# Three z buffers in turn from the y projections on, and operand groups of out and up made from z instead of DRAM

## The chip, the cores and the metric

The kernel runs on one core of a Trainium2 chip. The metric is device time in microseconds (us) of one execution; the median over several runs counts. An execution with the hardware profiler switched on gives the profile and the trace. The core's engines are TensorE (PE, with its weight loads as PEld), VectorE (DVE), ScalarE (ACT), GpSimd (POOL) and SyncE (SP). Each works through its own list of instructions in order, and they wait for one another with semaphores. SP, ACT and POOL also issue transfers (DMAs).

## The reference

One residual block over x of 512 tokens by 2048 channels, float32. What the change touches is the middle:

```python
y_m = hm @ w_branch_m                       # 1024 -> 2048
y_c = (cb * causal_dwconv(cc * ch, conv_w)) @ w_branch_c
merged = sigmoid(gm_pre) * y_m + sigmoid(gc_pre) * y_c
h = h + merged @ w_out                      # 2048 -> 2048

hn = rmsnorm(h, norm_ffn_g)
u = causal_dwconv(hn @ w_up, ffn_conv_w, ffn_conv_b)   # 2048 -> 2 * 5504
gate, val = jnp.split(u, 2, axis=-1)
h = h + (silu(gate) * val) @ w_down         # 5504 -> 2048
return rmsnorm(h, norm_out_g)
```

Before it stand the input projections (q, k, v, gates, the convolution's three inputs, gm_pre and gc_pre) and the mLSTM that gives hm.

## The kernel before

**Products and steps.** Channels lie on the 128 partitions, the 512 tokens along the row. Every matrix product is made of *items*. An item is one pair of output blocks (2 x 128 channels by 512 tokens) and has nq *steps*; a step takes in four blocks of 128 input channels, as two *cells* of two blocks each. A cell is a 2 x 2 block product (two input blocks, two output blocks or token halves of 256) done with seven block products instead of eight. Each block product is three matmuls, because every operand is split into a high part and a low rest (hi*hi + hi*lo + lo*hi). So a cell has 21 matmuls of 128x128 by 128x256 (lines 229 to 231), a step 42.

**Operand groups.** The activations of a cell are an *operand group*: `cell_task` loads two blocks from DRAM into a raw tile (L267, L268), makes the sums that the seven products need (t3, e, t4: L276, L281, L286; for up also the scaling by the norm's weights, L273 and L274), and writes the high part (L290, ScalarE) and the low rest (L293, VectorE) into one of eight group tiles. Weights go the same way in `weight_task`: a load of five transfers a step (three on SP, two adding ones on POOL at L204), two sums (L169, L174), high parts (L184, ScalarE) and low rests (`wl`, L188, VectorE). Raw tiles of weights and groups share a ring of six.

**Banks and z.** The seven products go to four banks of PSUM: three of the item's own set (two sets, in turn), and half of one bank, P_BANK, that both sets share. At an item's end `evac_first` (L245, ScalarE) copies P_BANK to a part of the item's buffer z, and in the next step four VectorE operations (L251 to L254) add up the rest there. z has two buffers, zs[0] and zs[1], that items take in turn:

```python
it.set = it.num % 2
it.z = zs[it.set]
```

The next item's first matmul into P_BANK waits for the copy before it.

**Posts.** What an item does with z afterwards is its post, in one to four pieces with a cost each. Pieces wait in a list, `posts`. Each step adds 5.04 us to a credit and takes off the VectorE work in it; at the end of a step the list is worked off as far as the credit goes, or at once when the first piece belongs to an *urgent* item. `flush(n)` issues all pieces up to item n. At the end of item n the main loop does this:

```python
flush(it.num - 2)
if it.pre:
    it.pre(it)
evac_first(it)
```

`pre` loads a second operand for the post into mA or mB (L628): gc_d for y_c, gm_d for y_m, xT for out, the residual for down; up has none. Stores to DRAM that a post makes are collected in `late` and issued by ScalarE (L146): right after a flush, else in the next step.

**Order.** Items follow in the order x (40 items of 4 steps, the input projections), y_c and y_m (8 items of 2 steps each), out (8 of 4), up (43 of 4), three parts of down (8 each, of 4, 3 and 3), and a last stage for the remaining channels. In each the last two items, and from y_c on the first two, are interleaved step by step. `phase` gives every group the step at which it must be complete (`spread`, relative to the stage's first step, and not before `after`); its sums run two steps earlier and its low rest one step earlier.

**The middle.** A y_c item's post multiplies z by the gate and stores it in mc_d. A y_m item's post multiplies z by its gate (L660), loads mc_d into the buffer z2 (L659), adds it (L663), negates the second half (L665: the products give minus the second block) and stores the pair in m_d. The groups of out load from m_d. An out item's post adds x (`residual`, L672 and L673), stores h_d and squares (L684); the squares are summed in z2 (L688), and after the last item summed over channels (L332) and turned into the norm's factor `rstd` (L340, L343). The groups of up load from h_d.

Of the kernel before, what the change touches and what calls it, by code (L numbers as in the profile page):

```python
# [11 lines left out]
AF = mybir.ActivationFunctionType  # L12
# [31 lines left out]
def kpair(c):  # L44

    q, r = divmod(c, 2)
    return 4 * q + r, 4 * q + 2 + r


class Item:  # L50


    def __init__(self, load, nq, xs, post, pre=None):
        self.load, self.nq, self.xs, self.post, self.pre = load, nq, xs, post, pre
        self.p1_start, self.urgent = True, False
        self.set = self.num = self.z = self.buf = None


class Task:


    def __init__(self, load, sums, hi, lo, ready=None):
        self.load, self.sums, self.hi, self.lo, self.ready = load, sums, hi, lo, ready
        self.wh = self.wl = None
        self.raw, self.cost, self.plain = None, (0.8, 2.05), False


@with_exitstack
def tile_block(ctx: ExitStack, tc: tile.TileContext, xT, w1, w_v0, w_v1, w_v2, w_bm, w_bc, w_out, w_up, w_down,
# [62 lines left out]
    gm_d, gc_d, mc_d, m_d, h_d, h2_d = (D_([KD, P, T], s) for s in ("gm_d", "gc_d", "mc_d", "m_d", "h_d", "h2_d"))  # L132
    a_d = D_([NF, P, T], "a_d")
    gates_d = D_([P, T], "gates_d")
    stored = set()
# [121 lines left out]
    def cell_task(xs, c, d, scale=None, key=None):  # L257

        k1, k2 = kpair(c) if isinstance(c, int) else c
        t = Task(None, None, None, None)  # L260

        def new_raw():
            t.raw = wp.tile([P, NW], F32, tag="raw", name=nm("xraw"), bufs=RAW)

        def load():
            new_raw()
            SP.dma_start(t.raw[:, 5 * SW:], d[k1])  # L267
            SP.dma_start(t.raw[:, :2 * SW], d[k2])  # L268

        def t3():  # L270
            x = slots(t.raw)
            if scale:
                A.activation(t.raw[:, 5 * SW:], t.raw[:, 5 * SW:], AF.Copy, scale=scale(k1))  # L273
                A.activation(t.raw[:, :2 * SW], t.raw[:, :2 * SW], AF.Copy, scale=scale(k2))  # L274

            V.tensor_sub(x[:, 2:4], x[:, 1:6:4], two(x[:, 6]))  # L276

        def e():

            x = slots(t.raw)  # L280
            V.scalar_tensor_tensor(x[:, 4], x[:, 3], -1.0, x[:, 1], op0=ALU.mult, op1=ALU.subtract)  # L281

        def t4():

            x = slots(t.raw)
            V.scalar_tensor_tensor(x[:, 6], x[:, 4], -1.0, x[:, 0], op0=ALU.mult, op1=ALU.subtract)  # L286

        def hi():
            t.act = actp.tile([P, 2 * NW], F32R, tag="act", name=nm("act"))
            A.activation(t.act[:, :NW], t.raw, AF.Copy)  # L290

        def lo():
            V.tensor_sub(t.act[:, NW:], t.raw, f(t.act[:, :NW]))  # L293
            t.raw = None
            xs[t.cell] = t.act
            t.act = None

        t.load, t.sums, t.hi, t.lo, t.new_raw = load, [t3, e, t4], hi, lo, new_raw
        t.cost = (1.35, 1.95)
        t.ready = (lambda: all(k in stored for k in key)) if key else None  # L300
        return t


# [349 lines left out]

    def ym_post(p):
        def post(it):
            j1, j2 = kpair(p)

            def one():
                SP.dma_start(sb_pair(z2), pair_ap(mc_d, j1, j2))  # L659
                V.tensor_mul(it.z, it.z, it.buf[:, :2 * T])  # L660

            def two_():
                V.tensor_add(it.z, it.z, z2)  # L663
                b = it.z[:, T:]
                A.activation(b, b, AF.Copy, scale=-1.0)  # L665
                store(pair_ap(m_d, j1, j2), sb_pair(it.z), ("m", p))
            return [(1.2, one), (1.2, two_)]
        return post

    def residual(it):  # L670
# [1 line left out]
        V.tensor_add(a, it.buf[:, :T], a)  # L672
        V.tensor_sub(b, it.buf[:, T:2 * T], b)  # L673

    acc = z2

    def out_post(p):
        def post(it):
            j1, j2 = kpair(p)

            def one():
                residual(it)
                store(pair_ap(h_d, j1, j2), sb_pair(it.z), ("h", p))
                A.activation(acc if p == 0 else it.buf[:, :2 * T], it.z, AF.Square)  # L684

            def two_():
                if p:
                    V.tensor_add(acc, acc, it.buf[:, :2 * T])  # L688
                if p == 7:
                    cols, rows_pe, rows_post = rows_stages(SIDE, rstd, mC)  # L690
                    side.append((lambda: sum_tokens(SIDE, acc, 2, 4, True, True), cols))
                    side.append((rows_pe, rows_post))
            return [(1.3, one), (1.2, two_)]
        return post

    def up_post(j):
# [38 lines left out]
    def add(items, inter):  # L735

        i = 0
        while i < len(items):
            n = 2 if i in inter else 1
            group = items[i:i + n]  # L740
            if n == 2:
                group[1].p1_start = False
            for it in group:
                it.num = len(items_all)
                it.set = it.num % 2
                it.z = zs[it.set]
                items_all.append(it)
            for q in range(group[0].nq):
                for it in group:
                    steps.append((it, q))  # L750
            i += n

    def phase(items, xs, cells, first_pair=True, last_pair=True, chained=False):

        inter = ({0} if first_pair else set()) | ({len(items) - 2} if last_pair else set())
        e = len(steps)
        add(items, inter)
        for n, t in enumerate(cells):
            t.cell, t.e, t.xs = n, e, xs
            if n == 7 and chained:  # L760
                for it in items_all[-len(items) - 2:-len(items)]:
                    it.urgent = True
            t.after = e + n - 2 if chained and n > 5 else 0
            t.spread = e + ((-4, -2, -1, 0, 2, 3, 5, 6) if items[0].nq > 2 else (-4, -2, 0, 1))[n]
            use = [s for s in range(e, len(steps)) if steps[s][1] == n // 2]
            t.first, t.last = use[0], use[-1]
            all_cells.append(t)
# [24 lines left out]
    def x_task(c):  # L792
# [20 lines left out]
        def hi():  # L813
# [7 lines left out]

    YC, HM, MM, HH = {}, {}, {}, {}
    phase([Item(tiles_load(w_bc, *kpair(p)), 2, YC, yc_post(p), load_pair(gc_d, *kpair(p))) for p in range(8)],
          YC, [cell_task(YC, c, yc_d, None, [("yc", k) for k in kpair(c)]) for c in range(4)])
    phase([Item(tiles_load(w_bm, *kpair(p)), 2, HM, ym_post(p), load_pair(gm_d, *kpair(p))) for p in range(8)],
          HM, [cell_task(HM, c, hm_d, None, [("hm", k) for k in kpair(c)]) for c in range(4)])
    phase([Item(tiles_load(w_out, *kpair(p)), 4, MM, out_post(p), load_pair(xT, *kpair(p))) for p in range(8)],
          MM, [cell_task(MM, c, m_d, None, [("m", c)]) for c in range(8)], chained=True)

    def up_load(j):  # L830
        return tiles_load(w_up, j, NF + j)

    phase([Item(up_load(j), 4, HH, up_post(j)) for j in range(NF)],
          HH, [cell_task(HH, c, h_d, g_ffn, [("h", c)]) for c in range(8)], chained=True)

    for c, (k0, nq) in enumerate(CHUNKS):
        AA = {}
# [67 lines left out]

    e_last = len(steps)
    t = last_act()
    t.cell, t.e, t.first, t.last, t.after, t.spread, t.xs = "x", e_last, e_last, e_last + 15, 0, 0, plain
    all_cells.append(t)
    n_main = len(steps)  # L910
    steps.extend((l, 0) for l in lasts)
# [5 lines left out]
    for n, t in enumerate(all_cells):  # L917
        if n < 8:
            k = t.cell // 2
        else:  # L920
            k = max(k, all_cells[n - 8].last + 3, t.e - 4, t.after, t.spread)
# [50 lines left out]
    def flush(upto):  # L972

        if posts and posts[0][2] <= upto:
            while posts and posts[0][2] <= upto:
                posts.popleft()[1]()
        flush_late()


    hf_tiles = {}  # L980
# [136 lines left out]
    for s in range(4, len(steps)):  # L1117
# [69 lines left out]
        for fn in dmas:  # L1187
            fn()
        if main and q == it.nq - 1:
            flush(it.num - 2)  # L1190
            if it.pre:
                it.pre(it)
            evac_first(it)
            ended.append(it)
        if t2 and not t2.plain:
            t2.hi(1)
# [1 line left out]
            fn()  # L1198
        if s >= 4 + hold:
            credit = min(credit, 2.5)  # L1200
            while posts and (credit > posts[0][0] / 2 or posts[0][2] in urgent or not main):
                cost, fn, _ = posts.popleft()
                credit -= cost
                fn()
# [84 lines left out]
```

## Time and profile before

| what | value |
|---|---|
| median of 3 runs | 2841.49 us (2838.44 to 2846.11) |
| the profiled execution | 2842.29 us, span 2840.5 us |
| TensorE busy | 2606.6 us, 92% of the span |
| VectorE busy | 2213.0 us, 78% |
| ScalarE busy | 1294.4 us, 46% |
| GpSimd busy | 853.8 us, 30% |
| granted TensorE clock, mean | 0.963 |
| moved by DMA | 642.36 MB, 226 GB/s |

The span is the time from the first to the last instruction; the execution's own time is a little longer. Busy time is a union over an engine's instructions. In the profile a group of instructions is a line, an engine, an operation and the tiles written and read; a wait is the idle time of an engine before an instruction, put down to what ended it.

### The profile page before, as it was taken

What the parts mean: (1) busy time and instruction counts of PE and PEld (TensorE: products, weight loads), DVE (VectorE), ACT (ScalarE), POOL (GpSimd) and SP (SyncE); (2) the same over time, 40 slices, a digit from 0 to 9 for tenths busy, and PEclk for the clock granted to TensorE, in tenths of its full rate; (3) what the DMA queues carried; (4) which work ended last, traced back from release to release, by engine and by line L of the source; (5) the groups of instructions that cost most, each with busy time, mean ns of one, the idle gap of its engine ahead of it and who ended that gap; (6) DMA issues with size and microseconds to landing.
All of it is one profiled execution on the core that took longest, in us unless ns stands there. A gap on an engine that the chain in (4) does not pass through costs nothing.

```text
span 2840.5 us, 55407 instructions
## 1 busy us (share of the span) xinstructions
PE 2606.6 (92%) x20868; PEld 2578.5 (91%) x20868; DVE 2213.0 (78%) x3360; ACT 1294.4 (46%) x1623; POOL 853.8 (30%) x1003
## 2 busy tenths in 40 slices
PE   7899999999999776689799999999999989979798
PEld 6899999999999776689799999999999979979797
DVE  5777768877777775777879988888888887767676
ACT  6444544455544332344545444444444443434343
POOL 3343323333332221132233333333333223222320
PEclk9999999999999888799999999999999999989899
DMA  7799998989898887798788888989888789889886
GB/s 189 177 236 239 235 245 204 248 214 251 225 240 224 229 238 217 205 259 232 220 211 223 221 225 221 227 216 227 221 223 223 203 227 258 235 236 251 225 244 202
DMA packets 504254, 642.36 MB, mean 226 GB/s; under 512 B 46849, under 2 KB 327425, under 8 KB 503985
## 3 DMA queue, kind: packets, MB, share of 16 engines
q1 hardware_dynamic: 326512, 451.78, 50.4%
q0 software_dynamic: 141536, 125.09, 30.1%
q10 hardware_dynamic: 35936, 61.95, 6.0%
q8 instruction: 163, 2.67, 0.4%
q14 instruction: 107, 0.87, 0.1%
HBM read 576.78 MB, written 61.87 MB: 225 GB/s over the span
## 4 chain that ended last, share of the span: by engine, by line
PE 71%; DMA 11%; DVE 9%; issue 3%; ACT 1%; POOL 0%; SPq 0%; DVEq 0%; POOLq 0%; ACTq 0%
PE bank L229 23%; PE bank L231 23%; PE bank L230 23%; DVE wl L188 3%; DMA h_d<-z 2%; DMA raw<-in_w_down_dram 2%; DVE act L293 2%; DMA z<-mc_d 1%; DMA raw<-in_w_out_dram 1%; DMA raw<-in_w_up_dram 1%; DMA mc_d<-z 1%; DMA raw<-in_w_dram 1%; DMA m_d<-z 1%; PE bank L512 1%; DMA raw<-in_w_bc_dram 1%
## 5 line engine op out<-in xcount | busy, mean ns | idle before, releaser
L229 PE MATMUL bank<-act,wh 128*128 128x256 f32 x6664 | 1928.5, 289 | 133.1 <-ACT z L245 118.2
L231 PE MATMUL bank<-act,wl 128*128 128x256 f32 x6664 | 1916.6, 288 | 52.9 <-DVE wl L188 52.8
L230 PE MATMUL bank<-act,wh 128*128 128x256 f32 x6664 | 1912.9, 287 | 2.3 <-DVE act L293 2.3
L229 PEld LDWEIGHTS bank<-act,wh 128*128 128x128 f32 x6664 | 1307.6, 196 | 142.5 <-ACT z L245 123.0
L184 ACT ACTIVATE wh<-raw 128x896 fp32r<-128x896 f32 x952 | 893.7, 951 | 1111.5 <-PE bank L230 723.7
L231 PEld LDWEIGHTS bank<-act,wl 128*128 128x128 f32 x6664 | 1307.4, 196 | 60.7 <-DVE wl L188 60.5
L230 PEld LDWEIGHTS bank<-act,wh 128*128 128x128 f32 x6664 | 1307.9, 196 | 6.4 <-DVE act L293 3.3
L188 DVE TENSOR_TENSOR wl<-raw,wh 128x896 fp32r<-128x896 f32 x952 | 1034.2, 1087 | 223.4 <-PE bank L231 159.4
L204 POOL DMA_DIRECT2D raw<-in_w_up_dram x344 | 298.9, 951 | 603.2 <-DMA raw<-in_w_up_dram 247.3
L204 POOL DMA_DIRECT2D raw<-in_w_dram x288 | 250.7, 947 | 552.6 <-DMA raw<-in_w_dram 305.3
L169 DVE TENSOR_TENSOR raw<-raw 128x256 f32<-128x256 f32 x476 | 199.6, 419 | 59.6 <-DMA raw<-in_w_down_dram 23.7
L204 POOL DMA_DIRECT2D raw<-in_w_down_dram x160 | 139.4, 986 | 346.4 <-DMA raw<-in_w_down_dram 195.1
L174 DVE TENSOR_TENSOR raw<-raw 128x256 f32<-128x256 f32 x476 | 199.0, 418 | 0.2
L251 DVE TENSOR_TENSOR z<-bank,z 128x512 f32<-128x512 f32 x131 | 90.0, 687 | 101.1 <-ACT z L245 99.5
L290 ACT ACTIVATE act<-xraw 128x1792 fp32r<-128x1792 f32 x52 | 88.3, 1698 | 80.8 <-DVE xraw L286 78.0
L245 ACT ACTIVATE z<-bank 128x256 f32<-128x256 f32 x131 | 48.5, 370 | 145.8 <-DMA h_d<-z 65.2
L293 DVE TENSOR_TENSOR act<-xraw,act 128x1792 fp32r<-128x1792 f32 x52 | 105.0, 2019 | 0.0
L204 POOL DMA_DIRECT2D raw<-in_w_out_dram x64 | 55.7, 971 | 156.4 <-DMA raw<-in_w_out_dram 95.8
L554 DVE TENSOR_TENSOR z<-z,rstd 128x1024 f32<-128x1024 f32 x83 | 101.0, 1218 | 0.0
L252 DVE TENSOR_TENSOR z<-bank,z 128x512 f32<-128x512 f32 x131 | 89.7, 684 | 0.3
L254 DVE TENSOR_TENSOR z<-bank,z 128x512 f32<-128x512 f32 x131 | 89.6, 684 | 0.0
L204 POOL DMA_DIRECT2D raw<-in_w_bm_dram x32 | 27.9, 991 | 112.2 <-DMA raw<-in_w_bm_dram 84.4
(202 smaller groups left out, 1240.6 us busy)
## 6 DMA issues: line engine op xcount, KB each, us to landing
raw<-in_w_up_dram SPq DMA_DIRECT2D x172, 512.0 KB, 5.6
raw<-in_w_dram SPq DMA_DIRECT2D x144, 512.0 KB, 5.9
raw<-in_w_up_dram SPq DMA_DIRECT2D x344, 128.0 KB, 4.2
raw<-in_w_up_dram POOLq DMA_DIRECT2D x344, 128.0 KB, 5.0
raw<-in_w_down_dram SPq DMA_DIRECT2D x80, 512.0 KB, 5.4
raw<-in_w_dram SPq DMA_DIRECT2D x288, 128.0 KB, 4.0
raw<-in_w_dram POOLq DMA_DIRECT2D x288, 128.0 KB, 5.1
raw<-in_w_down_dram SPq DMA_DIRECT2D x160, 128.0 KB, 4.0
```

The lines of the kernel that those rows point to most:

```text
L169: V.tensor_add(x[:, 6], x[:, 5], x[:, 0])
L174: V.tensor_add(x[:, 2], x[:, 6], x[:, 1])
L184: A.activation(seven(t.wh[r]), half(r), AF.Copy)
L188: V.tensor_sub(seven(t.wl[r]), half(r), seven(f(t.wh[r])))
L204: G.dma_start(at(i), a21, accum_op=ALU.add)
L229: PE.matmul(ps, h, xh, start=start, stop=False, skip_group_check=True)
L230: PE.matmul(ps, h, xl, start=False, stop=False, skip_group_check=True)
L231: PE.matmul(ps, l, xh, start=False, stop=last, skip_group_check=True)
L251: return [lambda: V.tensor_add(z[:, 0:4:3], b0, two(z[:, 1])), lambda: V.tensor_add(z[:, 1:3], b1, two(z[:, 3])), lambda: V.tensor_add(z[: ...
L252: lambda: V.tensor_add(z[:, 1:3], b1, two(z[:, 3])),
L293: V.tensor_sub(t.act[:, NW:], t.raw, f(t.act[:, :NW]))
L554: V.tensor_mul(sb_pair(it.z), sb_pair(it.z), two(rstd))
```

## The change

From item 40 on (y_c and all that follows; "y projections" are y_c and y_m) items take z2, zs[0] and zs[1] in turn, so z2 is no longer a scratch buffer there: the sum of squares moves to mC, at half its width.

At the end of an item the eviction comes first and the post of the item two before it after that, if the item has a `pre`; before the eviction only the post of the item three before is issued (two before for items up to 41). Inside `flush` late stores are issued only when a post was.

A group of out is now made by `direct_cell`: it loads mc_d into the raw tile and adds z of its y_m item from the buffer, the second block with its sign (z*-1 - b). The y_m post is the multiplication by the gate alone; m_d is gone. Groups 5 to 7 of up are scaled out of z of their out items; groups 0 to 4 still load h_d, which is stored as before. An item whose z is read this way is urgent, and a post is now issued at once when any waiting piece belongs to an urgent item. A group may be made at the earliest four steps after its item's last step.

The groups of y_m and of out are spread from 12 and 11 steps ahead of their stage (4 before).

```diff
+    def direct_cell(xs, c, it, d=None, scale=None, key=None):
+
+        t = cell_task(xs, c, d, None, key)
+        cell_t3, cell_load = t.sums[0], t.load
+        k1, k2 = kpair(c)
+
+        def load():
+            if d is not None:
+                cell_load()
+            else:
+                t.new_raw()
+
+        def t3():
+            assert it.done
+            a, b = t.raw[:, 5 * SW:], t.raw[:, :2 * SW]
+            if d is not None:
+                V.tensor_add(a, a, it.z[:, :T])
+                V.scalar_tensor_tensor(b, it.z[:, T:], -1.0, b, op0=ALU.mult, op1=ALU.subtract)
+            else:
+                A.activation(a, it.z[:, :T], AF.Copy, scale=scale(k1))
+                A.activation(b, it.z[:, T:], AF.Copy, scale=scale(k2))
+            it.z_read = True
+            cell_t3()
+
+        it.z_read = False
+        t.load, t.sums = load, [t3] + t.sums[1:]
+        t.cost = (2.7, 1.95) if d is not None else t.cost
+        t.after_end = it
+        return t
...
     def ym_post(p):
         def post(it):
-            j1, j2 = kpair(p)
-
-            def one():
-                SP.dma_start(sb_pair(z2), pair_ap(mc_d, j1, j2))
+            def fn():
                 V.tensor_mul(it.z, it.z, it.buf[:, :2 * T])
-
-            def two_():
-                V.tensor_add(it.z, it.z, z2)
-                b = it.z[:, T:]
-                A.activation(b, b, AF.Copy, scale=-1.0)
-                store(pair_ap(m_d, j1, j2), sb_pair(it.z), ("m", p))
-            return [(1.2, one), (1.2, two_)]
+                it.done = True
+            return [(1.2, fn)]
         return post
...
-    acc = z2
+    acc = mC
...
-                A.activation(acc if p == 0 else it.buf[:, :2 * T], it.z, AF.Square)
+                A.activation(it.buf[:, :2 * T], it.z, AF.Square)
+                it.done = True

             def two_():
                 if p:
-                    V.tensor_add(acc, acc, it.buf[:, :2 * T])
+                    V.tensor_add(acc, acc, it.buf[:, :T])
+                    V.tensor_add(acc, acc, it.buf[:, T:2 * T])
+                else:
+                    V.tensor_add(acc, it.buf[:, :T], it.buf[:, T:2 * T])
...
-                    side.append((lambda: sum_tokens(SIDE, acc, 2, 4, True, True), cols))
+                    side.append((lambda: sum_tokens(SIDE, acc, 1, 4, True, True), cols))
...
-                it.z = zs[it.set]
+                it.z = zs[it.set] if it.num < 40 else (z2, zs[0], zs[1])[(it.num - 40) % 3]
...
-    def phase(items, xs, cells, first_pair=True, last_pair=True, chained=False):
-
-        inter = ({0} if first_pair else set()) | ({len(items) - 2} if last_pair else set())
+    def phase(items, xs, cells, spread=(-4, -2, -1, 0, 2, 3, 5, 6), first_pair=True):
+
+        inter = ({0} if first_pair else set()) | {len(items) - 2}
...
-            t.cell, t.e, t.xs = n, e, xs
-            if n == 7 and chained:
-                for it in items_all[-len(items) - 2:-len(items)]:
-                    it.urgent = True
-            t.after = e + n - 2 if chained and n > 5 else 0
-            t.spread = e + ((-4, -2, -1, 0, 2, 3, 5, 6) if items[0].nq > 2 else (-4, -2, 0, 1))[n]
+            t.cell, t.xs, t.spread, t.after = n, xs, e + spread[n], 0
+            if t.after_end:
+                t.after_end.urgent = True
+                t.after = [i for i in range(e) if steps[i][0] is t.after_end][-1] + 4
...
+    phase(ym_items, HM, [cell_task(HM, c, hm_d, None, [("hm", k) for k in kpair(c)]) for c in range(4)],
+          (-12, -9, -6, -3))
...
+    phase(out_items, MM, [direct_cell(MM, c, ym_items[c], mc_d, None, [("mc", c)]) for c in range(8)],
+          (-11, -9, -7, -5, 0, 1, 2, 4))
...
+          HH, [direct_cell(HH, c, out_items[c], None, g_ffn) if c > 4 else
+               cell_task(HH, c, h_d, g_ffn, [("h", c)]) for c in range(8)], (-4, -2, -1, 0, 2, 3, 4, 5))
...
             while posts and posts[0][2] <= upto:
                 posts.popleft()[1]()
-        flush_late()
+            flush_late()
...
         if main and q == it.nq - 1:
-            flush(it.num - 2)
+            if it.num < 42:
+                flush(it.num - 2)
+            flush(it.num - 3)
+            assert it.num < 3 or getattr(items_all[it.num - 3], "z_read", True)
+            evac_first(it)
             if it.pre:
+                flush(it.num - 2)
                 it.pre(it)
-            evac_first(it)
             ended.append(it)
...
-            while posts and (credit > posts[0][0] / 2 or posts[0][2] in urgent or not main):
+            while posts and (credit > posts[0][0] / 2 or any(x[2] in urgent for x in posts) or not main):
```

More of the change, by code (lines that the diff above doesn't have):

```diff
@@ L54, in __init__ @@
         self.load, self.nq, self.xs, self.post, self.pre = load, nq, xs, post, pre
-        self.p1_start, self.urgent = True, False
+        self.p1_start, self.urgent, self.done = True, False, False
         self.set = self.num = self.z = self.buf = None
@@ L64, in __init__ @@
         self.wh = self.wl = None
-        self.raw, self.cost, self.plain = None, (0.8, 2.05), False
+        self.raw, self.cost, self.plain, self.after_end = None, (0.8, 2.05), False, None
 @with_exitstack
@@ L131, in tile_block @@
     so_d, cb_d, yc_d, hm_d = (D_([8, P, T], s) for s in ("so_d", "cb_d", "yc_d", "hm_d"))
-    gm_d, gc_d, mc_d, m_d, h_d, h2_d = (D_([KD, P, T], s) for s in ("gm_d", "gc_d", "mc_d", "m_d", "h_d", "h2_d"))
+    gm_d, gc_d, mc_d, h_d, h2_d = (D_([KD, P, T], s) for s in ("gm_d", "gc_d", "mc_d", "h_d", "h2_d"))
     a_d = D_([NF, P, T], "a_d")
@@ L683, in one @@
                 store(pair_ap(h_d, j1, j2), sb_pair(it.z), ("h", p))
-                A.activation(acc if p == 0 else it.buf[:, :2 * T], it.z, AF.Square)
+                A.activation(it.buf[:, :2 * T], it.z, AF.Square)
+                it.done = True
             def two_():
                 if p:
-                    V.tensor_add(acc, acc, it.buf[:, :2 * T])
+                    V.tensor_add(acc, acc, it.buf[:, :T])
+                    V.tensor_add(acc, acc, it.buf[:, T:2 * T])
+                else:
+                    V.tensor_add(acc, it.buf[:, :T], it.buf[:, T:2 * T])
                 if p == 7:
                     cols, rows_pe, rows_post = rows_stages(SIDE, rstd, mC)
-                    side.append((lambda: sum_tokens(SIDE, acc, 2, 4, True, True), cols))
+                    side.append((lambda: sum_tokens(SIDE, acc, 1, 4, True, True), cols))
                     side.append((rows_pe, rows_post))
-            return [(1.3, one), (1.2, two_)]
+            return [(1.3, one), (1.4, two_)]
         return post
@@ L823, in tile_block @@
     phase([Item(tiles_load(w_bc, *kpair(p)), 2, YC, yc_post(p), load_pair(gc_d, *kpair(p))) for p in range(8)],
[L824 to L828, printed above, removed]
+          YC, [cell_task(YC, c, yc_d, None, [("yc", k) for k in kpair(c)]) for c in range(4)], (-4, -2, 0, 1))
+    ym_items = [Item(tiles_load(w_bm, *kpair(p)), 2, HM, ym_post(p), load_pair(gm_d, *kpair(p))) for p in range(8)]
+    phase(ym_items, HM, [cell_task(HM, c, hm_d, None, [("hm", k) for k in kpair(c)]) for c in range(4)],
+          (-12, -9, -6, -3))
+    out_items = [Item(tiles_load(w_out, *kpair(p)), 4, MM, out_post(p), load_pair(xT, *kpair(p))) for p in range(8)]
+    phase(out_items, MM, [direct_cell(MM, c, ym_items[c], mc_d, None, [("mc", c)]) for c in range(8)],
+          (-11, -9, -7, -5, 0, 1, 2, 4))
     def up_load(j):
@@ L833, in tile_block @@
     phase([Item(up_load(j), 4, HH, up_post(j)) for j in range(NF)],
-          HH, [cell_task(HH, c, h_d, g_ffn, [("h", c)]) for c in range(8)], chained=True)
+          HH, [direct_cell(HH, c, out_items[c], None, g_ffn) if c > 4 else
+               cell_task(HH, c, h_d, g_ffn, [("h", c)]) for c in range(8)], (-4, -2, -1, 0, 2, 3, 4, 5))
     for c, (k0, nq) in enumerate(CHUNKS):
@@ L907, in tile_block @@
     t = last_act()
-    t.cell, t.e, t.first, t.last, t.after, t.spread, t.xs = "x", e_last, e_last, e_last + 15, 0, 0, plain
+    t.cell, t.first, t.last, t.after, t.spread, t.xs = "x", e_last, e_last + 15, 0, e_last - 4, plain
     all_cells.append(t)
@@ L920, in tile_block @@
         else:
-            k = max(k, all_cells[n - 8].last + 3, t.e - 4, t.after, t.spread)
+            k = max(k, all_cells[n - 8].last + 3, t.after, t.spread)
             if tasks[k]:
```

## The prediction

> **What bounds the kernel now.** I first read busy time and rate in stretches cut where one product of the block ends and the next begins. Columns: stretch, length, busy us (instructions) of TensorE, its weight load, VectorE, ScalarE and GpSimd, then granted clock, DMA share and GB/s.
>
> ```profile
> 928.10:1036.50 108.40, 87.19 (x672) 85.97 (x672) 82.86 (x120) 41.14 (x48) 27.54 (x32) 0.92 0.86 240
> 1036.50:1182.10 145.60, 97.50 (x672) 95.49 (x673) 97.29 (x135) 44.48 (x51) 26.19 (x30) 0.79 0.72 204
> 1182.10:1383.40 201.30, 169.94 (x1346) 167.51 (x1344) 149.11 (x211) 86.97 (x96) 55.97 (x65) 0.94 0.90 244
> 1383.40:2283.60 900.20, 880.91 (x7242) 877.64 (x7242) 790.70 (x1155) 437.27 (x532) 298.80 (x345) 0.99 0.87 220
> 2283.60:2473.30 189.70, 169.25 (x1345) 166.81 (x1345) 149.84 (x217) 80.63 (x87) 55.97 (x65) 0.96 0.91 242
> 2473.30:2627.50 154.20, 130.80 (x1008) 129.05 (x1008) 113.71 (x169) 57.26 (x62) 41.70 (x49) 0.92 0.89 241
> 2627.50:2775.40 147.90, 130.24 (x1010) 129.02 (x1011) 108.35 (x159) 53.26 (x62) 38.06 (x44) 0.93 0.87 236
> 2000.00:2200.00 200.00, 200.00 (x1669) 200.00 (x1668) 177.14 (x259) 96.81 (x120) 67.85 (x79) 1.00 0.88 221
> ```
>
> The last row, inside the up product, gives the pace of an unhindered TensorE: 200/1669 = 0.120 us a matmul, 5.04 us for a step of 42. The rows above it are y_c, y_m, out, up and the three parts of down. At that pace y_c and y_m (672 matmuls each) take 80.6 us, out 161.3, up 867, down 161.3 + 121 + 121 = 403.2. So y_c loses 27.8 us, y_m 64.9, out 40.0, up 33, down 88.6 of its 491.8. Next I asked what TensorE waits for in y_c, y_m, out, up, and in all of down, in this order (total us, times, longest):
>
> ```profile
> PE bank L229 <- ACT z L245: 13.8, 2, 8.7
> PE bank L231 <- DVE wl L188: 3.7, 3, 1.9
> ...
> PE bank L229 <- ACT z L245: 39.6, 6, 8.8
> PE bank L231 <- DVE wl L188: 8.5, 3, 4.1
> PE bank L229 <- DVE z L251: 3.7, 1, 3.7
> ...
> PE bank L229 <- ACT z L245: 17.2, 4, 10.0
> PE bank L231 <- DVE wl L188: 11.7, 6, 6.3
> ...
> PE bank L343 <- DVE mC L340: 5.7, 1, 5.7
> PE bank L229 <- ACT z L245: 3.7, 1, 3.7
> ...
> PE bank L229 <- ACT z L245: 40.0, 9, 7.3
> PE bank L231 <- DVE wl L188: 14.4, 12, 2.7
> PE bank L229 <- DVE z L251: 6.8, 3, 3.6
> ```
>
> One wait leads in every stage but up: L245, ScalarE's eviction of the shared bank, 114.3 us in 22 waits. The view of waits over the whole run says what L245 itself waits for: the store that still reads its z.
>
> ```profile
> ACT z L245 <- DMA h_d<-z: 65.2, 9, 10.4
> ...
> ACT z L245 <- DMA mc_d<-z: 39.7, 4, 12.7
> ...
> DVE z L663 <- DMA z<-mc_d: 24.2, 7, 5.7
> ...
> ACT z L245 <- DMA m_d<-z: 18.5, 4, 6.6
> ```
>
> The chain of waits in the second part of down shows the sequence (start, us, what):
>
> ```profile
> 2503.24 0.69 DVE z L672
> ...
> 2504.56 9.03 DMA h_d<-z
> 2513.67 0.39 ACT z L245
> 2514.11 0.58 PE bank L229
> ...
> 2515.12 0.21 PE bank L229
> ```
>
> The post of item n-2 is put off until item n ends; its store lands 9.03 us later, only then may item n's eviction write the same buffer, and TensorE resumes at 0.21 us a matmul. So a wait costs more than itself. In y_m the waits make 39.6 + 8.5 + 3.7 = 51.8 us and the loss is 64.9: L245 with its share of the slow clock is 39.6 x 64.9/51.8 = 50. The same ratio of loss to quoted waits gives 22 in y_c, 24 in out (40.0 over 28.9), 58 in down (88.6 over 61.2) and, at y_m's ratio, 5 in up: **159 us**, the most that a z buffer that is always free can bring.
>
> **Third buffer, eviction ahead of the post.** Item n now takes the buffer of n-3, whose post is issued at the latest when item n-1 has ended, one item sooner. An item lasts two to four steps, 10 to 20 us, longer than the 9.03 us of landing. The exception is the second item of an interleaved pair, which ends one step after the first: the store it needs leaves as its last step starts. TensorE feels a late eviction only 36 matmuls (4.3 us) after the item's last use of the bank, so about 5.04 + 4.3 = 9.3 us stand against 9.03 plus two residual adds of 0.69: nothing to 2 us for each first pair. What is left is set by VectorE or by the transfers, stage by stage.
>
> ```profile
> L276 DVE TENSOR_TENSOR xraw<-xraw 128x512 f32<-128x512 f32 x52 | 35.7, 687 | 26.5 <-ACT xraw L808 17.7 <-ACT xraw L274 8.8
> L281 DVE SCALAR_TENSOR_TENSOR xraw<-xraw 128x256 f32<-128x256 f32 x52 | 22.0, 423 | 1.1
> L293 DVE TENSOR_TENSOR act<-xraw,act 128x1792 fp32r<-128x1792 f32 x52 | 105.0, 2019 | 0.0
> L663 DVE TENSOR_TENSOR z<-z,z 128x1024 f32<-128x1024 f32 x8 | 9.8, 1226 | 24.2 <-DMA z<-mc_d 24.2
> L672 DVE TENSOR_TENSOR z<-mA,z 128x512 f32<-128x512 f32 x16 | 11.0, 686 | 0.0
> L604 DVE SCALAR_TENSOR_TENSOR z<-z,pcol 128x512 f32<-128x512 f32 x8 | 6.0, 752 | 8.7 <-ACT z L601 8.7
> ```
>
> **y_m.** Removed: eight adds L663 (9.8 us) with their waits for the load into z2, the negation on ScalarE (44.5 of 145.6 us busy here, so nothing by itself), the store and the load of m_d. Added to each out group: an add like L672 and a scalar_tensor_tensor like L604, 0.69 + 0.75 = 1.44 us; if the latter were as slow as two half-width ones (L281), 0.85. Five groups are now made in y_m (7.2 us), and by the new spread about one group more than before falls into it: 0.69 + 2 x 0.42 + 2.02 = 3.5 us. VectorE has 97.3 - 9.8 + 7.2 + 3.5 = 98 us against TensorE's 80.6 and becomes the bound. If it were busy for 100% of the stage that would last 98, at its share in up, 790.7/900.2 = 88%, 111. I take 95%, 104 us, nearer the first, since the loads and stores it stood for are gone: **gain 41**, bounds 34 and 47.
>
> **y_c.** The two L245 waits go (22 at most). It moved 240 x 108.4 = 26.0 MB; the groups of y_m are made some steps earlier, half a group more than now inside y_c (a group is 128 x 1024 x 4 bytes = 0.52 MB), 26.3.
>
> ```profile
> 1240.00:1340.00 100.00, 92.73 (x747) 91.92 (x748) 74.15 (x112) 40.60 (x47) 31.31 (x36) 0.97 0.95 257
> 1215.00:1265.00 50.00, 46.18 (x380) 45.58 (x379) 39.86 (x57) 22.26 (x23) 20.64 (x24) 1.00 1.04 275
> ```
>
> These stages hold 257 GB/s over 100 us and 275 over 50. At 257 y_c takes 102 us, at 275 96: **gain 7**, bounds 2 and 17.
>
> **out.** L245 goes with 24 us. Groups 5 to 7 are still split in its first four steps, 4.7 to 5 us each with the new adds beside 5.04 a step for TensorE, so part of the waits on wl (L188) stays. Bounds: 14 if these grow by half of what L245 frees, 28 if only 12 us are lost in the stage. **Gain 22.** As a check, the three stages moved 26.0 + 29.7 + 49.1 = 104.8 MB; without eight stores and eight loads of m_d it is 96.4, 375 us at 257 GB/s, 80 fewer than their 455.3; my 70 fits under that.
>
> **down.** 58 at most. Its 45.9 + 37.2 + 34.9 = 118 MB need 459 us at 257 GB/s, 33 fewer than now, and 429 at 275. **Gain 37**, nearer the lower one as VectorE is full at each part's start; bounds 26 (pairs still waiting) and 52.
>
> **up.** One L245 wait with its slow clock: **gain 5**. Groups 5 to 7 come from z, with the same scaling on ScalarE and no VectorE work less; group 6 now shares a step with the chain behind L340, whose 5.7 us can grow by its 1.5 us of sums. With posts allowed to lag three items, -3 to 8. The sum of squares costs two adds of 0.69 for one of 1.23, and the column sums are four fewer: under 2 us in all, behind TensorE.
>
> **Queues.** SP issues in order, and the weights behind a load of m_d stood with it (y_m, then out):
>
> ```profile
> SPq L267 <- DMA m_d<-z: 15.7, 3, 5.7
> ...
> SPq L267 <- DMA m_d<-z: 9.4, 3, 5.9
> ```
>
> Loads of mc_d wait for no late store, so this goes; I count it inside y_m and out. The groups moved forward take slots of the six raw buffers earlier, leaving four steps, 20 us, of weights ahead, more than the landings seen. Stores left over at an item's end now leave one step later on ScalarE's queue; nobody reads them soon.
>
> Sum: 41 + 7 + 22 + 37 + 5 = 112. The profiled execution took 2842.3 us (span 2840.5 and 1.8 around it), 0.8 above the median of the runs: 2842.3 - 112 = **2730**. Own range of this case, not all bounds at once: 2700 to 2765.
>
> A ceiling of another kind stands on a page: the Trainium skill, HBM Reference, Specifications, has a core that streams alone at about 425 GB/s. By it down would need 118/425 = 278 us of transfers, under TensorE's 403, and the sum would rise to some 145. The trace disagrees for this mix: share 1.04 at 275 GB/s. The Trainium skill, TensorE: Matmul & The Clock Gate, Part 1, halves the clock after an idle window of about 3.4 us and gives it back after as long a busy one, about 1.7 us a wait: 22 x 1.7 = 37 where my ratio has 159 - 114 = 45; by it the 159 would be 151.
>
> **Rivals.**
> - *All of L245's cost goes.* For it: VectorE idles inside these waits. Against: its 98 us in y_m. 2842 - 159 = **2683**.
> - *The transfers cap it.* Down already moves 236 to 242 GB/s. If 242 is the ceiling, 96.4 MB take 398 us (gain 57) and 118 take 488 (gain 4): **2781**. Against: 257 and 275 above.
> - *The wait only moves on*, so that the change doesn't do what it says. With more in flight the stores land later, and the third buffer is waited for as the second was. What is left is the m_d path, 18.5 + 24.2 us: **2799**. Against: an item more of time, 10 us at the shortest.
> - *Slower.* The multiply of all y_m items and the posts of out items 5 to 7 now run in the step after the item. VectorE, in order, may stand there for a load just issued (L628), with the weight splits behind it and TensorE behind those.
>
> ```profile
> DMA to landing us min/median/max: 3.5/6.3/11.3
> ```
>
> Eleven items at the longest landing, 11 x 11.3 = 124 us, against the 112: 2842 + 12 = **2854**. It decides from about 10 us of VectorE wait an item. Against: the load leaves at the item's end, and four eviction operations plus a step's splits stand before the multiply.
>
> **How the numbers follow.** Likeliest 0.60, all of it 0.10, transfer cap 0.17, wait moves on 0.06, slower 0.05, no change 0.02. Less than 0.3% (8.5 us), about what this measurement can tell, counts as same. Faster 0.93, same 0.02, slower 0.05. The range runs from 2690, short of the full recovery, to 2795, past the transfer cap; about 0.17 is left out.
>
> **What would show it.** Right: L245 all but gone from TensorE's waits, y_m near 104 us with VectorE above 90% of it and the clock above 0.9, down near 455 at about 257 GB/s. Wrong: L245 still waiting for stores (the wait moved on); VectorE at L660 waiting for gm_d (slower); waits for raw transfers grown by tens of us (the cap).

## The result, and the profile after

The changed kernel takes **2732.94 us** (median of 4 runs, 2728.89 to 2736.55) against 2842.79 for the kernel before in the same series: ratio 0.961, 95% interval 0.960 to 0.963. Predicted were 2730 us and a gain of 112; measured are 110. The profiled execution took 2736.55 us, span 2734.8.

The same stretches as before the change, cut where one product ends and the next begins (columns as in the prediction: stretch, length, the engines' busy us, granted clock, DMA share, GB/s):

```profile
927.40:1035.30 107.90, 88.84 (x672) 87.21 (x673) 92.03 (x131) 43.34 (x50) 31.06 (x36) 0.92 0.90 252
1035.30:1131.50 96.20, 85.21 (x675) 83.99 (x674) 89.11 (x131) 39.12 (x44) 23.21 (x28) 0.96 0.92 261
1131.50:1311.60 180.10, 166.73 (x1346) 164.29 (x1344) 149.38 (x219) 83.80 (x93) 55.12 (x64) 0.98 0.91 245
1311.60:2216.20 904.60, 880.73 (x7235) 877.62 (x7235) 791.20 (x1157) 438.20 (x533) 299.65 (x345) 0.98 0.86 217
2216.20:2403.00 186.80, 169.66 (x1345) 167.43 (x1345) 149.82 (x217) 80.63 (x87) 55.64 (x65) 0.96 0.92 245
2403.00:2538.00 135.00, 124.42 (x1008) 122.79 (x1008) 113.54 (x169) 57.39 (x62) 41.56 (x48) 0.99 0.97 273
2538.00:2669.50 131.50, 126.06 (x1010) 125.31 (x1011) 108.46 (x159) 53.33 (x62) 38.35 (x44) 0.96 0.96 269
```

Read against the prediction's terms (us):

| stage | before | after | gained | predicted |
|---|---|---|---|---|
| y_c | 108.4 | 107.9 | 0.5 | 7 |
| y_m | 145.6 | 96.2 | 49.4 | 41 |
| out | 201.3 | 180.1 | 21.2 | 22 |
| up | 900.2 | 904.6 | -4.4 | 5 |
| down | 491.8 | 453.3 | 38.5 | 37 |
| sum | | | 105.2 | 112 |

The span fell by 105.7 us, so the middle holds the whole gain. What TensorE still waits for in y_c, y_m, out, up, and in all of down:

```profile
PE bank L231 <- DVE wl L188: 11.2, 5, 5.7
PE bank L229 <- ACT z L245: 6.2, 2, 4.7
...
PE bank L231 <- DVE wl L188: 9.5, 5, 4.0
PE bank L229 <- ACT z L245: 1.5, 1, 1.5
...
PE bank L231 <- DVE wl L188: 8.4, 7, 2.1
...
PE bank L229 <- ACT z L245: 0.7, 1, 0.7
...
PE bank L373 <- DVE mC L370: 10.6, 1, 10.6
PE bank L231 <- DVE wl L188: 9.0, 6, 2.4
...
PE bank L229 <- ACT z L245: 1.8, 1, 1.8
...
PE bank L231 <- DVE wl L188: 21.6, 15, 4.0
...
PE bank L229 <- ACT z L245: 4.9, 2, 2.8
```

The eviction L245 held TensorE for 114.3 us in these stages before; now it is 6.2 + 1.5 + 0.7 + 1.8 (in up) + 4.9, about 15. What leads now is wl, VectorE's low rests of the weights. L245's own waits, over the whole run, have shrunk from 65.2 us for h_d stores and 39.7 for mc_d stores to this, and m_d is gone:

```profile
ACT z L245 <- DMA h_d<-z: 11.5, 2, 6.1
...
ACT z L245 <- DMA mc_d<-z: 4.8, 1, 4.8
```

Three stages fell outside the bounds of the forecast: y_c gained nothing, y_m gained 8 us more than forecast, and up lost 4 us. The experiments ask which part of the change earns what, and where these terms went. Each run's ratio is to the kernel before, with its 95% interval; stage lengths are from each run's profile.

### The profile page after: what moved, and what is told of

Its sections match the earlier page's. It is cut to its first block, busy times and chain, and to the rows that moved or that the text cites. A ratio compares the mean times of both kernels' runs of the same rounds, so it can differ in the third digit from the quotient of the medians.

```text
span 2734.8 us, 55343 instructions
## 1 busy us (share of the span) xinstructions
PE 2582.4 (94%) x20860; PEld 2555.7 (93%) x20860; DVE 2214.5 (81%) x3376; ACT 1289.4 (47%) x1615; POOL 854.5 (31%) x1003
## 4 chain that ended last, share of the span: by engine, by line
PE 75%; DVE 9%; DMA 7%; issue 3%; ACT 1%; POOL 0%; SPq 0%; DVEq 0%; ACTq 0%; POOLq 0%
PE bank L231 24%; PE bank L229 24%; PE bank L230 24%; DVE wl L188 3%; DMA raw<-in_w_down_dram 2%; DMA raw<-in_w_bc_dram 1%; DVE act L293 1%; DMA raw<-in_w_out_dram 1%; DMA h_d<-z 1%; DVE raw L169 1%; PE bank L542 1%; DMA raw<-in_w_up_dram 1%; DVE z L252 1%; DVE z L251 0%; DVE raw L174 0%
## 5 line engine op out<-in xcount | busy, mean ns | idle before, releaser
L174 DVE TENSOR_TENSOR raw<-raw 128x256 f32<-128x256 f32 x476 | 199.0, 418 | 0.2
L293 DVE TENSOR_TENSOR act<-xraw,act 128x1792 fp32r<-128x1792 f32 x52 | 105.0, 2019 | 0.0
L245 ACT ACTIVATE z<-bank 128x256 f32<-128x256 f32 x131 | 48.2, 368 | 25.6 <-DMA h_d<-z 11.5
L253 DVE TENSOR_TENSOR z<-bank,z 128x256 f32<-128x256 f32 x131 | 55.6, 425 | 4.5
```

The source lines that it names most:

```text
L174: V.tensor_add(x[:, 2], x[:, 6], x[:, 1])
```

## The experiments

### The third buffer, from up on

```diff
-                it.z = zs[it.set]
+                it.z = zs[it.set] if it.num < 64 else (z2, zs[0], zs[1])[(it.num - 64) % 3]
...
-            flush(it.num - 2)
-            if it.pre:
-                it.pre(it)
-            evac_first(it)
+            if it.num < 64:
+                flush(it.num - 2)
+                if it.pre:
+                    it.pre(it)
+                evac_first(it)
+            else:
+                flush(it.num - 3)
+                evac_first(it)
+                if it.pre:
+                    flush(it.num - 2)
+                    it.pre(it)
```

> The kernel before with one part of the change: from the up product on (item 64) items take z2, zs[0], zs[1] in turn, and there the eviction L245 stands ahead of the post of the item two before. Groups, m_d and everything up to the end of out are as before. Theory (the stores' landing is what L245 waits for, and a third buffer is enough): down goes from 491.8 to about 455 us, up from 900.2 to 895, and the time from 2842 to about 2801. Rival (the stages are held by transfers or by the wait moved on): down stays above 480 and the time above 2828. TensorE's waits on L245 in down should fall from 40.0 us to under 8.

Measured: 2805.04 us, ratio 0.987 (0.983 to 0.990). The three parts of down, and TensorE's waits in them:

```profile
2279.90:2467.20 187.30, 168.40 (x1345) 165.96 (x1345) 149.81 (x217) 80.48 (x87) 55.84 (x65) 0.97 0.91 244
2467.20:2605.00 137.80, 128.10 (x1009) 126.88 (x1009) 113.63 (x169) 57.50 (x62) 41.77 (x49) 0.95 0.96 267
2605.00:2736.20 131.20, 125.81 (x1010) 124.92 (x1011) 108.24 (x159) 53.28 (x62) 38.01 (x44) 0.96 0.96 271
```

```profile
PE bank L231 <- DVE wl L188: 22.6, 15, 4.0
...
PE bank L229 <- ACT z L245: 5.1, 2, 2.9
```

Down lasts 456.3 us, up 899.0, and L245 keeps 5.1 us. The third buffer is nearly all of the gain in down (35.5 of 38.5), and the rival of a wait that only moves on falls: L245 went from 40.0 to 5.1, wl from 14.4 to 22.6. The edit also puts the eviction ahead of the post. That is not what earns it: with three buffers and the old order (a run below) down lasts 454.3 us. The part of the change ahead of up was not tried this way: there z2 is the scratch of the y_m posts and of the sum of squares, and it is free to be a third buffer only when these are gone.

### Direct groups alone, early and late

The changed kernel with two buffers and the old order at an item's end (group 5 of up from h_d, since two buffers overwrite its z):

```diff
-                it.z = zs[it.set] if it.num < 40 else (z2, zs[0], zs[1])[(it.num - 40) % 3]
+                it.z = zs[it.set]
...
-          HH, [direct_cell(HH, c, out_items[c], None, g_ffn) if c > 4 else
+          HH, [direct_cell(HH, c, out_items[c], None, g_ffn) if c > 5 else
...
-            if it.num < 42:
-                flush(it.num - 2)
-            flush(it.num - 3)
...
+            flush(it.num - 2)
...
+            if it.pre:
+                it.pre(it)
             evac_first(it)
-            if it.pre:
-                flush(it.num - 2)
-                it.pre(it)
```

> The changed kernel with two z buffers and the old order at an item's end (post of the item two before, its load, then the eviction); groups of out come from z and mc_d, groups 6 and 7 of up from z, group 5 of up from h_d (with two buffers its z is overwritten too early). Theory: only the m_d path is gained. y_m keeps the waits for mc_d stores of the last y_c items (31 us in the waits of L245 before) and goes from 145.6 to about 112 us, y_c stays near 108, out gains 10 to 190, down stays at 490: about 2800. If the third buffer were all, the time would stay above 2830; if the direct groups were all, it would come near 2735.

Measured: 2828.98 us, ratio 0.995 (0.993 to 0.997), a far smaller gain than expected. y_m did fall, to 97 us, but y_c rose to 148:

```profile
930.30:1078.30 148.00, 96.62 (x673) 94.80 (x674) 93.36 (x131) 43.65 (x50) 32.69 (x38) 0.82 0.74 201
1078.30:1175.40 97.10, 85.52 (x674) 83.70 (x673) 89.97 (x132) 40.14 (x45) 22.64 (x26) 0.96 0.83 231
```

In its y_c, TensorE waits for the eviction seven times (before: twice, 13.8 us). The eviction waits five times for stores of mc_d (before: once, 8.4 us), and for two of gc_d, the stores of the last input projections, much as before (11.4 us):

```profile
PE bank L229 <- ACT z L245: 48.0, 7, 9.6
...
ACT z L245 <- DMA mc_d<-z: 45.3, 5, 10.3
...
ACT z L245 <- DMA gc_d<-z: 13.8, 2, 7.0
```

The y_m groups, made earlier, are the suspect: their work is taken off the credit, so the y_c posts would no longer be issued on credit but at the end of the item two after, right before the eviction that needs the buffer. The next run puts these groups back.

```diff
-          (-12, -9, -6, -3))
+          (-4, -2, 0, 1))
```

> Two buffers, the old order at an item's end and direct groups, as in the run with direct groups only, but the groups of y_m made where they were before the change (4 and 2 steps ahead, at the start, one after). That run lost 40 us in y_c (148.0 against 108.4) and won 48 in y_m. Theory (groups made early use up the credit, so that each y_c post is put off to the end of the item two after and each eviction waits for its store): y_c comes back to about 108, y_m takes the waits for the last y_c stores and lasts about 122, the time is about 2812. Rival (the waits in y_c come from the direct groups themselves, made in y_m): y_c stays near 148.

Measured: 2809.71 us, ratio 0.989 (0.985 to 0.992).

```profile
927.00:1036.50 109.50, 87.86 (x675) 86.44 (x673) 82.54 (x119) 41.17 (x48) 27.81 (x32) 0.92 0.86 239
1036.50:1157.40 120.90, 93.38 (x673) 91.37 (x674) 100.09 (x143) 42.58 (x47) 27.83 (x32) 0.87 0.79 217
```

y_c is back at 109.5 and y_m lasts 120.9, both as expected. In y_c the eviction waits once for a store of mc_d, where the run before waited five times:

```profile
ACT z L245 <- DMA mc_d<-z: 8.7, 1, 8.7
```

So the early groups bring the waits into y_c, not the direct ones; that the credit is the link between the two is read from the program's rule and was not tried by itself. With the y_m groups in their old place direct groups are worth 34 us (2843.52 to 2809.71), the third buffer from up on 37 (2841.60 to 2805.04). The whole change is worth 110. The 39 us left are what the third buffer adds in y_c, y_m and out beside direct groups, with the early y_m groups: from this run to the changed kernel y_c shrinks by 1.6 us, y_m by 24.7 and out by 7.2 (187.3 to 180.1). What a third buffer would bring there without direct groups stays open, as z2 is not free then.

### The early y_m groups in the changed kernel

The same edit of the spread, made in the changed kernel with its three buffers:

> The changed kernel with the groups of y_m made where they were before (4 and 2 steps ahead, at the stage's start and one after, instead of 12, 9, 6 and 3 ahead). Theory (y_c gained nothing because these groups moved into it): y_c falls from 107.9 to about 101, y_m rises from 96.1 to about 102, the time is within 5 us of the changed kernel's 2733. Rival (y_c is held by its first steps and late loads of weights whatever is made in it): y_c stays at 106 or more and y_m rises all the same, 2739.

Measured: 2741.28 us, ratio 0.964 (0.961 to 0.968).

```profile
926.10:1023.00 96.90, 84.95 (x673) 83.72 (x673) 82.76 (x120) 40.93 (x48) 27.67 (x32) 0.96 0.98 271
1023.00:1129.70 106.70, 89.75 (x672) 87.02 (x673) 98.92 (x142) 42.09 (x47) 27.48 (x32) 0.93 0.86 242
```

y_c is 11.0 us shorter, y_m 10.5 longer, both 4 to 5 us more than expected. VectorE's busy time says why: 82.8 and 98.9 us here, 92.0 and 89.1 in the changed kernel. Early groups move 9 us of VectorE's work from y_m to y_c, and in both runs y_c lasts 17% longer than VectorE is busy, and y_m 8%. With three buffers the early place costs and brings the same in these two stages (203.6 us against 204.1). The medians of the whole time are 8 us apart and the intervals of the ratios overlap; the two spans profiled differ by only 1.2 us, so where the 8 us would lie isn't shown.

### The order at an item's end

```diff
-            if it.num < 42:
-                flush(it.num - 2)
-            flush(it.num - 3)
+            flush(it.num - 2)
+            if it.pre:
+                it.pre(it)
...
             evac_first(it)
-            if it.pre:
-                flush(it.num - 2)
-                it.pre(it)
```

> The changed kernel with three buffers, but at an item's end the old order: post of the item two before, load of its second operand, eviction last. Theory: the order counts for little where the buffer is free; the eviction stands behind a store whose issue waits for VectorE, some 1 to 2 us at a third of the 67 items with a load: 2745, 10 above the changed kernel. If the order were what removes the waits, L245 would be back in TensorE's waits with 50 us or more and the time above 2790.

Measured: 2734.54 us, ratio 0.962 (0.958 to 0.965): no difference from the changed kernel. Of the waits of this run, over the whole of it:

```profile
PE bank L231 <- DVE wl L188: 49.2, 36, 4.1
PE bank L229 <- ACT z L245: 34.3, 15, 4.7
```

and of the changed kernel:

```profile
PE bank L231 <- DVE wl L188: 66.5, 44, 5.7
...
PE bank L229 <- ACT z L245: 19.0, 8, 4.7
```

The old order brings L245 back for 15 us and takes 17 off wl: 83.5 in all against 85.5. The changed kernel run again (below) waits 59.4 us for wl and 18.5 for L245, so 7 of the 17 are within the spread of one kernel. Evicting ahead of the post mostly changes the name of the wait; why wl gives way was not taken apart.

### Where up lost its time

The chain of waits of the changed kernel at the second step of up (start, us, what):

```profile
1340.60 0.43 DVE raw L174
1341.10 0.95 ACT wh L184
1342.05 0.61 ACT xraw L322
1342.66 0.62 ACT xraw L323
1343.31 0.69 DVE xraw L276
1344.00 1.93 DVE act L293
1345.93 0.35 DVE xraw L281
1346.30 0.42 DVE xraw L286
1346.84 0.21 ACT ny L348
...
1348.28 0.69 DVE mC L370 x3
1349.01 2.07 PE bank L373 x2
```

Group 6 is scaled on ScalarE (L322, L323) and summed (L276, L281, L286) in front of the norm's column chain (L348 to L370), for whose diagonal TensorE waits at L373: 10.6 us where the kernel before waited 5.7. There the same chain is shorter (the line numbers of the norm differ by 30):

```profile
1412.10 0.42 DVE raw L174
...
1415.56 0.21 ACT ny L318
...
1417.74 2.08 PE bank L343 x2
```

From the weights' sum L174 to the column chain (ny) it is 3.5 us there and 6.2 here: group 6 costs 2.8 of the 4.9 us that the wait grew by. Two edits try it.

First, groups 6 and 7 back to their old step:

```diff
-               cell_task(HH, c, h_d, g_ffn, [("h", c)]) for c in range(8)], (-4, -2, -1, 0, 2, 3, 4, 5))
+               cell_task(HH, c, h_d, g_ffn, [("h", c)]) for c in range(8)], (-4, -2, -1, 0, 2, 3, 5, 6))
```

> The changed kernel with groups 6 and 7 of up one step later, as before the change. Theory (up lost 4 us because the sums of group 6 now stand in VectorE's list ahead of the norm's chain that TensorE waits for): that wait falls from 10.6 us to about 6, up from 904.5 to about 899, the time from 2733 to about 2728. Rival (the wait comes from the eviction's or the sums of squares' order): it stays at 10 us and up at 904.

Measured: 2728.36 us, ratio 0.960 (0.957 to 0.962); up 899.4 us, and the wait:

```profile
1311.20:2210.60 899.40, 879.34 (x7234) 875.80 (x7234) 790.66 (x1157) 437.80 (x533) 299.48 (x346) 0.99 0.87 218
...
PE bank L373 <- DVE mC L370: 7.8, 1, 7.8
```

Second, an empty stage between the column chain and the matmul:

```diff
                     side.append((lambda: sum_tokens(SIDE, acc, 1, 4, True, True), cols))
+                    side.append((noop, noop))
                     side.append((rows_pe, rows_post))
```

> The changed kernel with TensorE's matmul of the norm's row put off by one step (an empty stage between the column chain and it). Theory: the 10.6 us wait for the diagonal vanishes, but VectorE is full there, so a part comes back as waits on wl: up goes from 904.5 to about 896, the time to about 2725. Rival (VectorE's backlog is all of it and only changes its name): up stays above 902.

Measured: 2724.95 us, ratio 0.958 (0.956 to 0.961); up 898.9 us.

```profile
PE bank L373 <- DVE mC L370: 3.3, 1, 3.3
```

Both confirm the place. The first takes 2.8 us off the wait, just what group 6 cost, though 4.6 were expected; up is 5.2 us shorter, so not all of that is this wait. The second takes 7.3 us off the wait; wl in up is 10.7 us, against 9.0 in the changed kernel and 7.3 when it was run again. In that second run of the changed kernel up lasts 902.7 us and the wait 9.3, so a difference of 2 us in up is within the spread of one kernel; both edits lie beyond it. The whole times of these two runs, 2728.36 and 2724.95, are to be read against 2732.94 and, when it was run again, 2729.24.

### The two waits left in y_c

```diff
-            if it.num < 42:
+            if it.num < 40:
                 flush(it.num - 2)
```

> The changed kernel, but the post of the item two before is issued ahead of the eviction only up to item 39 instead of 41. Theory (the two y_c waits of L245 that are left, 6.2 us with 8 us of lost time, come from ScalarE making the last gates of the input projections before it evicts): L245 in y_c falls below 3 us, y_c from 107.9 to about 101, the time to about 2727. Rival (VectorE and the late weights bound y_c anyway): y_c stays above 106.

Measured: 2728.64 us, ratio 0.960 (0.958 to 0.962). L245 in y_c fell as expected, the stage less:

```profile
PE bank L231 <- DVE wl L188: 10.5, 5, 4.7
PE bank L229 <- ACT z L245: 2.8, 1, 2.8
```

y_c lasts 105.5 us, 2.4 fewer and not 7: nearer to the view in which VectorE and the late weights bound the stage. With the same edit the two runs at the end of the next part have y_c at 103.3 and 104.7 us, the changed kernel run again 107.3: some 2 to 4 us are real, and neither view has all of it.

### Together

The changed kernel once more, with the next two beside it:

> The changed kernel itself, as the measure for the two runs beside it on the same chip: 2733, ratio 0.961.

Measured: 2729.24 us (2726.93 to 2735.11), ratio 0.959 (0.957 to 0.961). With the empty stage and the flush up to item 39:

> The changed kernel with the norm's row matmul put off by one step and the old flush only up to item 39. Theory (two separate waits, at both ends of the middle, so the gains add): 8 us from the first and 3 to 4 from the second: 2722, some 11 below the changed kernel. If VectorE were the bound through the whole middle and each wait only moved, it would stay within 3 us of the changed kernel.

Measured: 2722.31 us (2720.13 to 2724.42), ratio 0.956 (0.954 to 0.958): 7 us under the changed kernel, where 11 were expected. With groups 6 and 7 of up late as well:

> The same with groups 6 and 7 of up one step later as well. Both edits on the norm's chain address the same wait of 10.6 us, of which the gap left 3.3; theory: they don't add, 1 to 3 us more at most, 2720. If they add in full (8 and 5 us), 2717.

Measured: 2717.56 us (2713.38 to 2723.14), ratio 0.955 (0.953 to 0.957). The wait at L373 falls to 0.4 us, up lasts 896 us:

```profile
1304.30:2200.20 895.90, 877.28 (x7234) 872.76 (x7234) 790.73 (x1157) 437.87 (x533) 299.38 (x345) 0.99 0.87 219
```

Its runs all lie below those of the changed kernel beside it, 12 us in the medians; it beats both kernels. Whether the late groups add to the empty stage is not settled: the 4.8 us between the last two medians are inside the spread of their runs, and up itself is only some 2 us shorter (898.2 to 896.0).

## Why the prediction was right

**The sum.** Right, and in part by luck. Profiled run against profiled run the gain is 105.7 us of the 112 (the medians say 110). The errors of y_c and y_m cancel; what is short is mostly up's miss of 9 us.

**What bounds it, and the third buffer.** Right. L245's waits for stores went with a buffer more: shown by the run with the third buffer from up on, down 491.8 to 456.3. The pair exception was right in place and a little small: what TensorE still waits for L245 in down, twice, 4.9 us in all and 2.8 at most, comes after the second item of a first pair (put at nothing to 2).

**y_m and y_c.** The working of y_m found the right bound, VectorE: 98 us of its work, busy for 95% of the stage. With the groups in their old place the stage has 98.9 us of it and lasts 106.7, 93%. The step that failed is "by the new spread about one group more than before falls into it", and "half a group more" in y_c. Counted by their low rests (L293), y_m holds five groups before, six with the groups in their old place and four in the changed kernel; y_c holds four, four and six. The early groups carry 9 us of VectorE work out of y_m into y_c. (A smaller slip: of the eight adds L663 that were taken off y_m, only five, 6.1 us, stood there; three stood in out.) So y_m gained 49.4 instead of 41, above the upper bound of 47, and y_c 0.5 instead of 7, below the lower of 2. That the two errors cancel is luck: 48 predicted for both stages, 49.9 measured. The transfers at 257 GB/s, which I took for the bound of y_c, were not it: with late groups y_c moves 271 GB/s and lasts 96.9 us. Its DMA share is 0.98 there, so whether the transfers hold it at that rate is open.

**out.** 22 predicted, 21.2 measured; L245 fell from 17.2 to 0.7 us, and wl kept 8.4 of 11.7, as argued.

**up.** Gain 5, measured -4.4. The wait of L245 went as expected (3.7 to 1.8 us). The mis-sized term is the growth of the chain behind L340, put at 1.5 us of sums: 5.7 became 10.6. The sums alone were priced. The chain of waits shows 1.2 us of scaling on ScalarE and 1.5 of sums ahead of it, 2.8 us with the gaps between them. The other 2.1 of the 4.9 us lie ahead of the weights' sum L174 and were not taken apart. The run with groups 6 and 7 late takes 2.8 us off the wait and 5.2 off up.

**down.** 37 against 38.5 is right in the sum, but not for the reason in each part. The first part gained only 2.9 us: L245's 9.8 us went, and wl rose from 7.3 to 13.1; why was not taken apart. The second and third gained 19 and 16 us and moved 273 and 269 GB/s over 135 and 131 us: the 257 GB/s used as a mark was no ceiling. Whether 273 is one, at a DMA share of 0.97, no run shows.

**The rivals.** The transfer cap at 242 GB/s is refuted by these rates. The slower case did not come: no wait of VectorE for gm_d loads shows in y_m. The full recovery of 159 us did not come, though not for the reason that its counter-argument gave, VectorE in y_m: there 49.4 of its 50 us were gained. It failed in y_c (0.5 of 22), where the early groups add VectorE work, in down (38.5 of 58), where wl rose from 14.4 to 21.6 us, and in up (-4.4 of 5).

**Clock and transfers.** The slow clock left with the waits, as reckoned: in y_m the granted clock rose from 0.79 to 0.96 as the waits fell from 51.8 to 11.0 us. But the price of the slow clock is not in proportion to the wait, as the ratios took it. Take waits that stand alone, with no other above 0.3 us among the 60 matmuls on either side, and the time of the 60 matmuls behind each, less 60 x 0.120 us. In the kernel before a wait of 2.5 us (at 1140.2) then costs 1.6 us beyond itself, one of 5.1 us (981.5) 2.3 and one of 8.7 us (959.7) 1.4; all ten from 2.5 to 8.8 us cost 1.4 to 2.3. In the changed kernel a wait of 2.4 us (1489.9) costs 1.6, one of 2.1 us (2443.8) 0.1 and one of 1.5 us (1039.2) 0.1. So in these traces a long wait costs about as much extra as a short one, once it costs anything, and a wait that is only shortened can keep its price. By this y_c's two waits were worth 13.8 + 1.4 + 2.3, some 17 us, not 22.

The 425 GB/s that the Trainium skill, HBM Reference, Specifications, states for a core alone was not approached: the most over a stage of the changed kernel is 273 GB/s, at a DMA share of 0.97.

## What to carry to other kernels

When an engine waits for a store that still reads a buffer, price the wait with the slow clock that follows it, add a buffer, and then count the work of the next engine by stage: here that sum told y_c and y_m apart, and the waits removed did not. A budget that puts work off until it is forced can turn early work elsewhere into a chain of waits: moving groups ahead cost y_c 39 us with two buffers (148.0 against 109.5), and about 20 in all. And work moved one step ahead of a short dependent chain can lengthen the wait on that chain's end, here from 5.7 to 10.6 us; look for what stands behind it in the same list.

## What the runs showed that I had not expected

The order in which ScalarE evicts and posts, which the change turned round, is worth nothing measurable once the buffer is free (2734.54 against 2732.94 us): the waits trade 15 us of L245 for 10 to 17 us of wl. Transfers held 273 GB/s for 135 us; the kernel before held 257 over 100 us and 275 over 50.
